# One planner for all engines up to the sweeps; plain fp32 adaLN, tokens turned before they are scaled, the gate third beside heads 1 to 3

## The chip, the core and the metric

The kernel runs on one core of a Trainium2 chip. The metric is the device time of one execution in microseconds, the median of several runs. TensorE (PE) multiplies matrices out of SBUF into PSUM; VectorE (DVE), ScalarE (ACT) and GpSimd (POOL) work on elements, and GpSimd can't read PSUM; SyncE (SP) issues the DMAs. Each engine takes its instructions strictly in the order in which they were issued to it, and waits for the others by semaphores.

## The reference

One layer of a hybrid encoder, for a prompt of 1024 tokens and a sample of 256, D = 1024. All is fp32.

```python
mod = c @ w_ada + b_ada
shift, scale, gate = jnp.split(mod[:, None, :], 3, axis=-1)
h = rms_norm(x, norm_g) * (1.0 + scale) + shift
p = h @ w_in                                   # (tokens, 11 D + 16)
cb, cc, cx, cz, q, k, v, o, mz, gpre, gmerge = split_combined(p)
y_conv = cb * centred_dwconv3(cc * cx, conv_w, conv_b) * jax.nn.silu(cz)
...  # h_fwd, h_bwd: chunkwise mLSTM over q, k, v with the gates gpre, in both directions, 4 heads
hm = hm * lax.rsqrt(jnp.mean(hm * hm, axis=-1, keepdims=True) + EPS)   # hm = h_fwd + h_bwd
y_m = jax.nn.sigmoid(o) * hm * jax.nn.silu(mz)
g_conv, g_mlstm = jnp.split(jax.nn.sigmoid(gmerge), 2, axis=-1)
merged = g_conv * (y_conv @ w_proj_conv) + g_mlstm * (y_m @ w_proj_mlstm)
return x + gate * (merged @ w_out)             # and a last rms_norm
```

## The kernel before

A large product is made of three products of rounded parts: each operand x is split into a high part H (a cast to fp32r) and a low part L = x - H, and HH, HL and LH are added up in PSUM.

**The start.** Five blocks of 128 tokens are loaded, then the first two thirds of `w_ada` in eight blocks of 1 MB (`wa`, five buffers), then the other five token blocks. ScalarE sums the squares (L355), VectorE scales each block by its root mean square (L362), TensorE turns it to channels x tokens (`turn`, L372). `ada(kt)` splits a block of `w_ada` into parts (ScalarE L411, VectorE or GpSimd L412) and multiplies them by the conditions (L425); the last quarter is multiplied as plain fp32 (L418). The result gives a scale `s1` and a shift `shf` for each channel. Tokens 0 to 383 are turned before these are known; the other groups are turned later, and scaled as they leave PSUM (`affine`, L378 and L380).

**Strassen products.** The input projection is done by a seven-product scheme of blocks: K in two halves, tokens in two halves (`b11`, `b21`, `b12`, `b22`), columns in pairs of 128. The moving operands are b11, b21, b22 and four combinations t1 to t4 (made at L1022, split at L1041 and L1044); the weights are combined on VectorE (`comb`, L513) and split on ScalarE (L292) and GpSimd (L293). One product is 24 matrix instructions of 320 columns (`product`, L471). VectorE adds each result to partial sums (`plus`, L543). There are 308 products: eight pairs of merge gates (the first eight products of them are taken ahead, as "corners"), head 0, eight pairs of o and mz (`og_pair`), sixteen of the convolution, heads 1 to 3. `run` is the order by hand: product p, then the turns and deferred steps of the product before (`turn_one`, `deferred`), the taking up of its result, the weights of product p + 2. Three accumulators (`accx`) are in PSUM.

**Beside the products.** `gate_inputs` and `recurrences` make the mLSTM's scalars. `weights` (20 tiles of exponentials) and `thirds` run beside the og pairs. `thirds` makes the last third of adaLN, the output gate, on VectorE: 128 multiply-adds of 128 x 128 (L966), from weight blocks (`wg`, one buffer) and a bias row (`gacc`), with a sum on TensorE and a row stored for each of eight parts. Keys and values are turned to tokens x channels and stored.

**The sweeps.** The mLSTM runs over heads in two directions. Here a planner, `Board`, already orders all engines: each operation has an engine, a duration written in the code, what it reads and writes and a step; `order` takes again and again the engine that can start first, and of its operations those that can start within 0.25 the one of the lowest step. The product `y_conv @ w_proj_conv` is cut into 32 units (`Filler`) that fill TensorE's gaps; `PACE` says how many units are given out up to each step.

**The output.** For each half of the tokens `merge` makes the mLSTM's projection and adds the two, and `finish` multiplies by `w_out` in quarters of 256 columns (L1668 to L1670), adds the residual (`residual`) and norms (`norm_out`).

## Time and profile before

| | us |
|---|---|
| median of 3 runs (lowest to highest) | 1767.04 (1766.39 to 1769.45) |
| the profiled execution's own time | 1767.08 |
| its span, first to last instruction | 1765.1 |
| TensorE busy | 1681.6 |
| VectorE busy | 958.9 |
| GpSimd busy | 696.7 |
| ScalarE busy | 620.4 |

The stages in the profiled execution: adaLN up to 53 us, Strassen products from 53 to 1229, with og pairs from 371, the convolution from 595 and heads 1 to 3 from 989; the sweeps from 1229 to 1527; the output from there on. A stretch's busy time is to be read beside its length: what TensorE lacks there is what an edit of that stretch can win at most. Durations of matrix instructions overlap, so the time of one is read from the distance of two starts.

### The profile page before, as it was taken

To read this page: it belongs to the slowest core of one execution; us is meant where nothing else is said; L and a number is where in the kernel's file an instruction comes from. 1 tells how busy PE (TensorE), PEld (TensorE's weight loads), DVE (VectorE), ACT (ScalarE), POOL (GpSimd) and SP (SyncE) were. 2 spreads that over 40 slices of the span, in tenths; PEclk is the share of its full clock that TensorE was granted. 3 is DMA by queue.
4 is the path that set the end of the run, shared out by engine and by line. 5 is a ranking of instruction groups with operands and counts; after the bars stand their busy time and mean duration, and the time that the engine had idled before them with its cause. 6 is when DMAs were issued, how large, how long until landed. Compare 5 with 4: busy or idle time off the path is not lost.

```text
span 1765.1 us, 29030 instructions
## 1 busy us (share of the span) xinstructions
PE 1681.6 (95%) x11182; PEld 1620.9 (92%) x11182; DVE 958.9 (54%) x1703; ACT 620.4 (35%) x1243; POOL 696.7 (39%) x533
## 2 busy tenths in 40 slices
PE   4879999999988999999999999999999999899997
PEld 1679999999887999999999999999888889799997
DVE  6884333257788455555554433322247677556546
ACT  6552332223444322222222222222246565334223
POOL 2453333334454466666666633333210101223322
PEclk9889999999999999999999999999999999899999
DMA  7223332313554322222222243336878864763731
GB/s 298 84 74 119 108 101 96 106 56 106 150 162 136 97 67 78 58 64 71 66 78 66 89 123 103 96 123 230 295 230 273 271 188 142 252 222 121 255 101 72
DMA packets 213694, 239.59 MB, mean 136 GB/s; under 512 B 12356, under 2 KB 172340, under 8 KB 212532
## 3 DMA queue, kind: packets, MB, share of 16 engines
q1 hardware_dynamic: 213556, 237.74, 42.4%
q8 instruction: 88, 1.44, 0.3%
q14 instruction: 50, 0.41, 0.1%
HBM read 169.46 MB, written 68.23 MB: 135 GB/s over the span
## 4 chain that ended last, share of the span: by engine, by line
PE 63%; DVE 3%; DMA 1%; issue 1%; ACT 1%; POOL 0%; SPq 0%; DVEq 0%; ACTq 0%; POOLq 0%
PE accx L471 36%; PE qc L1281 3%; PE u L1299 3%; PE accd L1454 2%; PE accd L1455 2%; PE accd L1456 2%; PE accd L1669 2%; PE accd L1670 2%; PE accd L1668 2%; PE acc L1523 2%; PE acc L1524 2%; PE acc L1525 2%; PE misc L1382 1%; PE misc L1342 1%; DVE gacc L966 1%
## 5 line engine op out<-in xcount | busy, mean ns | idle before, releaser
L543 DVE TENSOR_TENSOR q<-accx,q 128x640 f32<-128x640 f32 x288 | 233.4, 821 | 477.4 <-PE accx L471 404.7
L293 POOL TENSOR_TENSOR wl<-comb,wh 128x512 fp32r<-128x512 f32 x176 | 236.8, 1347 | 486.8 <-ACT wh L292 439.6
L293 POOL TENSOR_TENSOR wl<-raw,wh 128x512 fp32r<-128x512 f32 x168 | 234.9, 1403 | 162.7 <-ACT wh L292 150.4
L471 PE MATMUL accx<-half,wh 128*128 128x320 f32 x1408 | 266.0, 311 | 6.9 <-ACT wh L292 5.2
L292 ACT CAST wh<-comb 128x512 fp32r<-128x512 f32 x176 | 108.6, 620 | 371.8 <-DVE comb L513 284.9
L471 PEld LDWEIGHTS accx<-half,wh 128*128 128x128 f32 x1408 | 221.4, 189 | 8.5 <-ACT wh L292 5.5
L471 PE MATMUL accx<-half,wl 128*128 128x320 f32 x704 | 161.0, 310 | 0.8 <-POOL wl L293 0.8
L292 ACT CAST wh<-raw 128x512 fp32r<-128x512 f32 (+1 forms) x184 | 119.5, 654 | 71.2 <-PE accd L1670 17.9
L1484 POOL TENSOR_TENSOR wl<-raw,wh 128x512 fp32r<-128x512 f32 x28 | 35.9, 1288 | 234.8 <-ACT wh L1483 234.8
L632 ACT ACTIVATE q<-q,zero 128x640 f32<-128x640 f32 x80 | 66.4, 830 | 172.0 <-DVE q L543 153.7
L471 PEld LDWEIGHTS accx<-half,wl 128*128 128x128 f32 x704 | 118.0, 188 | 1.4 <-POOL wl L293 1.4
L1669 PE MATMUL accd<-wl,mH 128*128 128x256 f32 x320 | 89.6, 280 | 0.1
L1670 PE MATMUL accd<-wh,mL 128*128 128x256 f32 x320 | 89.5, 280 | 0.0
L1668 PE MATMUL accd<-wh,mH 128*128 128x256 f32 x320 | 89.5, 280 | 0.0
L471 PE MATMUL accx<-b10H,wh 128*128 128x320 f32 x352 | 82.5, 316 | 7.0 <-ACT q L1070 5.9
L471 PE MATMUL accx<-t2H,wl 128*128 128x320 f32 x352 | 81.4, 313 | 5.6 <-POOL wl L293 5.6
L471 PE MATMUL accx<-b00H,wh 128*128 128x320 f32 x352 | 82.0, 314 | 2.3 <-DVE half L380 2.3
L471 PE MATMUL accx<-t2H,wh 128*128 128x320 f32 x352 | 81.7, 313 | 2.0 <-ACT wh L292 2.0
L471 PE MATMUL accx<-b10H,wl 128*128 128x320 f32 x352 | 81.2, 312 | 1.1 <-POOL wl L293 1.1
L471 PE MATMUL accx<-t3H,wl 128*128 128x320 f32 x352 | 80.4, 310 | 1.1 <-POOL wl L293 1.1
L471 PE MATMUL accx<-t3H,wh 128*128 128x320 f32 x352 | 80.5, 310 | 1.0 <-ACT wh L292 1.0
L471 PE MATMUL accx<-b11H,wl 128*128 128x320 f32 x352 | 80.3, 309 | 1.1 <-POOL wl L293 1.1
(301 smaller groups left out, 4233.2 us busy)
## 6 DMA issues: line engine op xcount, KB each, us to landing
raw<-in_w_in_dram SPq DMA_DIRECT2D x96, 256.0 KB
raw<-in_w_in_dram SPq DMA_DIRECT2D x44, 512.0 KB
th_dr<-q SPq DMA_DIRECT2D x32, 320.0 KB
th<-th_dr SPq DMA_DIRECT2D x32, 320.0 KB
wa<-in_w_ada_dram SPq DMA_DIRECT2D x8, 1024.0 KB
raw<-in_w_proj_conv_dram SPq DMA_DIRECT2D x16, 512.0 KB
k<-kn_dr SPq DMA_DIRECT2D x64, 128.0 KB
raw<-in_w_proj_mlstm_dram SPq DMA_DIRECT2D x16, 512.0 KB
```

Of the source, the lines that this page charges most:

```text
L292: A.copy(wh[:], src)
L293: eng.tensor_tensor(out=wl[:], in0=src, in1=fp(wh[:]), op=ALU.subtract)
L471: PE.matmul(acc[:, q, 0:TQ], st_[:, k, :], m_[:, q * TQ:(q + 1) * TQ], start=k == 0 and n == 0, stop=k == 3 and n == 2)
L543: V.tensor_tensor(out=two(dst), in0=ps, in1=two(t), op=ALU.add)
L632: A.activation(out, in_, AF.Tanh, bias=zero[:, 0:1], scale=0.5)
L1281: PE.matmul(pq[:, 0:HD + 2], qTs[i][:, kd, c * P:(c + 1) * P], C[:, kd, :], start=kd == 0, stop=kd == 1)
L1299: PE.matmul(pu[:, db, 0:HD + 2], k[:, db * P:(db + 1) * P], wv[:], start=True, stop=True)
L1454: PE.matmul(accs[q][:, :TQ], wh, yH, start=kt == 0, stop=False)
L1484: op("POOL", 1.36, lambda wh=wh, wl=wl, src=src: G.tensor_tensor(out=wl[:], in0=src(), in1=fp(wh[:]), op=ALU.subtract), r=[raw, wh], w=[wl])
L1668: PE.matmul(pd, sH, ws[0][:, k, :], start=kt == 0, stop=False)
L1669: PE.matmul(pd, sH, ws[1][:, k, :], start=False, stop=False)
L1670: PE.matmul(pd, sL, ws[0][:, k, :], start=False, stop=kt == KT - 1)
```

## The change

The planner now orders all engines from the first load on, in pieces with one plan each (`board.play` is called at the end of each, and forgets what it has played); `run`, `defer`, `settle` and the lists of stores are gone. `phase` and `go` record the same 308 products, each in four operations (one for each block of K). `prep` records the weights of a product with the step of two products before (five for the first twelve).

- *The start*: all ten token blocks are loaded before `w_ada`, normed, and turned without scale and shift into the operands' buffers. `w_ada` isn't split: each block is multiplied as plain fp32 (32 products of 512 columns). Then `affine` scales and shifts in place in SBUF, and `both_parts` and `combine` make the seven operands, while the corners run (two of b11, two of b21, then pairs).
- *By tokens*: keys and values are turned as soon as the plan has them.
- *The gate third* (`thirds`) moves from the og pairs to heads 1 to 3: it is recorded at each seventh product, its sum six products later. The heads' ring of result tiles has six tiles instead of eight.
- *Sweeps*: units from 18 on (22 before) have low priority, and `PACE` gives 30 units before step 50 and the last two from it on.
- *Output*: `w_out` in halves of 512 columns: half as many matrix instructions, twice as wide, and the same for the operations of `residual`.

```diff
-                wah = ad.tile([P, D], F32R, tag=f"wah{h}", name="wah")
-                wal = ad.tile([P, D], F32R, tag=f"wal{h}", name="wal")
-                A.copy(wah[:], was[kt][:, hs])
-                (G if h == 0 and kt % 2 == 0 else V).tensor_tensor(out=wal[:], in0=was[kt][:, hs], in1=fp(wah[:]), op=ALU.subtract)
-                parts[h] = wah, wal
...
+        self.ops = []
+        for key in list(self.places):
+            self.places[key] = [b for b in self.places[key] if b.open]
+            if not self.places[key]:
+                del self.places[key]
...
+        def turn_x(i, cs):
+            t0, tn = cs[0] * P, len(cs) * P
+            for kt in range(KT):
+                px = buf(psP, [P, 512], F32, "px", 2)
+                dst, d0 = xt[kt // 4, t0 // TH2][kt % 4], t0 % TH2
+
+                def turn(px=px, kt=kt):
+                    for j, c in enumerate(cs):
+                        PE.transpose(px[:, j * P:(j + 1) * P], xin[c][:, kt * P:(kt + 1) * P], ident[:])
+
+                op("PE", .11 * len(cs), turn, r=[xin[c] for c in cs], w=[px])
+                f = (A.copy, V.tensor_copy)[kt % 2]
+                op(("ACT", "DVE")[kt % 2], .5, lambda f=f, px=px, dst=dst, d0=d0: f(dst[:, d0:d0 + tn], px[:, :tn]),
+                   r=[px], w=[(dst, i)])
...
+        def ada(kt):
+            for h in range(2):
+                for j in range(2):
+                    op("PE", .88, lambda h=h, j=j: PE.matmul(
+                        pada[h][0:4, j, :], cz4[:, kt, :], was[kt][:, h * D + j * 512:h * D + (j + 1) * 512],
+                        start=kt == 0, stop=kt == KT - 1), r=["cz4", was[kt]], w=[("pada", h, j)])
...
+        for i, cs in enumerate(GROUPS):
+            load_x(cs)
+        for kt in range(KT):
+            load_ada(kt)
...
+    def affine(j, l, ks=range(4)):
+        for i in ks:
+            x, kt = xt[j, l][i], 4 * j + i
+            for a, b, smp in ((0, TH2, 0),) if l == 0 else ((0, T0 - TH2, 0), (T0 - TH2, TH2, 1)):
+                sc, sh = s1[:, kt, smp:smp + 1], shf[:, kt, smp:smp + 1]
+                act = i % 2 if l == 0 else smp
...
+    def prep(k):
+        if k < len(todo) and k not in made:
+            board.step = k - (5 if k < 12 else 2)
+            made[k] = todo[k][0].prep(todo[k][1])
...
+        for k_ in range(4):
+            op("PE", .84, lambda k_=k_: mm(k_), r=[*w, *((MOV_B[mv][part][k_]) for part in range(2))] + ([acc] if k_ else []),
+               w=[acc])
+        for b in w:
+            b.open = False
+        take(acc)
...
+            op("PE", .11 * jn, turn, r=[t.tok], w=[pv])
+            op("ACT", .2 + .1 * jn, lambda j0=j0, jn=jn, pv=pv: A.copy(vt()[:, j0 * P:(j0 + jn) * P], pv[:, :jn * P]),
+               r=[pv], w=[(vt.b, j0)])
...
+            op("DVE", .95, first, r=ru, w=rc)
+            op("DVE", 2.0, left, r=ru + rc, w=rc)
+            op("DVE", 2.0, right, r=ru + rc, w=rc)
...
+        for k in range(8):
+            if k == 2:
+                board.step = 3
+                affine(1, 1)
+                affine(0, 1)
+
+                board.step = 4
+                both_parts("b22", B22, (0, 0, 0, 0))
+                combine(B22, B22, B12, 0)
+                board.step = 7
+                combine(B12, B12, B11, 1)
+                board.step = 5
+                combine(B11, B22, B11, 0, ALU.add)
+                both_parts("t2", B11, (0, 0, 0, 0))
+                board.step = 6
+                both_parts("t3", B22, (0, 1, 0, 1))
+                board.step = 8
+                combine(B21, B21, B11, 0)
+                singles("t1")
+                both_parts("t1", B12, (1, 1, 1, 1))
+                singles("t4")
+                both_parts("t4", B21, (0, 0, 0, 0))
...
-            side = [weights(gw), thirds(gw)]
-            run(ends[8], side)
...
+    def thirds(pool, n):
+
+        acc = buf(pool, [P, 2, P], F32, "acc", 2)
+        op("POOL", .45, lambda: G.memset(acc[:], 0.0), w=[acc])
+        for s in range(2):
+            load(1, lambda s=s: acc[0:1, s], b_ada[0:1, 2 * D + n * P:2 * D + (n + 1) * P], [], [acc])
+        for j in range(2):
+            raw = buf(pool, [P, 4, P], F32, "wg", 1)
+            load(256, lambda raw=raw: raw[:], wada[:, 4 * j:4 * j + 4, 2 * D + n * P:2 * D + (n + 1) * P], (), [raw])
+            for i in range(4):
+                def use(i=i, j=j, raw=raw):
+                    for s in range(2):
+                        k = 8 * s + 4 * j + i
+                        V.scalar_tensor_tensor(out=acc[:, s], in0=raw[:, i], scalar=cols[:, k:k + 1], in1=acc[:, s],
+                                               op0=ALU.mult, op1=ALU.add)
+
+                op("DVE", .85, use, r=[raw, acc], w=[acc])
...
+            if n < KT and m == 0:
+                third[n] = thirds(gw, n)
+            if n < KT and m == 6:
+                third[n]()
+            go(k)
...
-    PACE = [min(4 + s, 12) if s < 10 else 12 + (s - 9) * 4 // 7 if s < 17 else 16 if s < 21 else min(17 + (s - 21) * 15 // 29, 32)
+    PACE = [min(4 + s, 12) if s < 10 else 12 + (s - 9) * 4 // 7 if s < 17 else 16 if s < 21 else min(17 + (s - 21) * 13 // 28, 30) if s < 50 else 32
...
-                op("PE", .88, lambda part=part: mm(part), r=ops + ([acc] if part else []), w=[acc], low=u >= 22,
+                op("PE", .88, lambda part=part: mm(part), r=ops + ([acc] if part else []), w=[acc], low=u >= 18,
...
+        def residual(pd, j, n2):
+            ns = slice(n2 * 512, (n2 + 1) * 512)
+            t = ep.tile([P, 4 * P], F32, tag="t", name="t")
             V.tensor_tensor(out=t[:], in0=pd, in1=gbc[0 if c0 + j < 8 else 1][:, ns], op=ALU.mult)
             V.tensor_tensor(out=ob[:, j, ns], in0=ob[:, j, ns], in1=t[:], op=ALU.add)
             A.activation(t[:], ob[:, j, ns], AF.Square, bias=zero[:, 0:1], scale=1.0,
-                         accum_out=ssq[:, j, n4:n4 + 1])
+                         accum_out=ssq[:, j, n2:n2 + 1])
...
+        for n2 in range(2):
+            ws = [weights_o(n2, half) for half in range(2)]
+            if last and n2 == 1:
```

## Rows read from the trace of the kernel before

**Rows 1.** The page: the span, and the engines' busy time with its share of the span.

```profile
span 1765.1 us, 29030 instructions
...
PE 1681.6 (95%) x11182; PEld 1620.9 (92%) x11182; DVE 958.9 (54%) x1703; ACT 620.4 (35%) x1243; POOL 696.7 (39%) x533
```

**Rows 2.** Busy time by stretch, the whole kernel: the stretch and its length in us, busy us (and instructions) of each engine, granted clock as a share of full speed, DMA share, GB/s.

```profile
5.00:24.00 19.00, 6.59 (x24) 3.94 (x24) 8.17 (x27) 11.56 (x19) 0.06 (x1) 1.00 0.99 406
...
53.00:131.00 78.00, 61.89 (x356) 58.53 (x355) 63.85 (x77) 42.30 (x68) 39.20 (x23) 0.85 0.16 52
...
131.00:455.00 324.00, 324.00 (x2221) 320.08 (x2220) 145.99 (x240) 99.01 (x170) 117.68 (x92) 1.00 0.34 101
455.00:580.00 125.00, 110.79 (x700) 101.04 (x699) 105.02 (x172) 51.36 (x115) 63.18 (x53) 1.00 0.54 153
580.00:990.00 410.00, 410.00 (x2798) 410.00 (x2797) 217.80 (x242) 103.37 (x169) 256.71 (x179) 1.00 0.22 68
990.00:1004.00 14.00, 12.07 (x71) 11.55 (x70) 6.56 (x6) 4.94 (x8) 8.57 (x6) 0.88 0.55 189
1004.00:1229.00 225.00, 224.65 (x1561) 224.26 (x1559) 70.31 (x95) 57.75 (x117) 78.41 (x62) 1.00 0.40 128
...
1240.00:1518.00 278.00, 270.41 (x1584) 246.43 (x1583) 174.62 (x574) 145.48 (x377) 37.23 (x29) 1.00 0.72 230
1518.00:1532.00 14.00, 6.71 (x27) 5.83 (x26) 5.75 (x13) 4.18 (x9) 2.00 (x2) 0.63 0.79 248
...
1586.00:1643.00 57.00, 57.00 (x487) 57.00 (x486) 36.07 (x56) 23.59 (x52) 21.17 (x22) 1.00 0.38 121
...
1756.00:1765.00 9.00, 0.00 (x0) 0.00 (x0) 3.91 (x13) 1.62 (x4) 0.72 (x1) 0.75 0.44 176
```

**Rows 3.** The chain that ended last, in order of time, heads 1 to 3: start us, us, what.

```profile
1008.18 10.56 PE accx L471 x72
```

**Rows 4.** TensorE in order of time, 85 to 135 us: start us, us to the end of the last of them, what; in brackets the idle time before and what ended it.

```profile
118.46 1.44 PE L471 MATMUL accx<-half,wh 128*128 128x320 f32 x4 [5.24 <-ACT wh L292]
...
131.12 0.45 PE L471 MATMUL accx<-t2H,wh 128*128 128x320 f32 x2
```

**Rows 5.** TensorE in order of time, from the start to the turns of the last two token groups (columns as in rows 4).

```profile
36.09 1.09 PE L425 MATMUL accx<-wal,cst 128*4 128x512 f32 x4
37.02 1.09 PE L425 MATMUL accx<-wah,cst 128*4 128x512 f32 x4
...
46.02 1.88 PE L418 MATMUL accx<-wa,cz 128*4 128x512 f32 x4
47.83 0.63 PE L425 MATMUL accx<-wah,cst 128*4 128x512 f32 x2
48.30 0.62 PE L425 MATMUL accx<-wal,cst 128*4 128x512 f32 x2
...
53.11 0.54 PE L471 MATMUL accx<-b00H,wh 128*128 128x320 f32 x2
...
73.25 2.34 PE L372 MATMUL accx<-ident,xin 128*128 128x128 f32 x15
```

**Rows 6.** ScalarE in order of time, 0 to 60 us (columns as in rows 4).

```profile
7.55 1.28 ACT L355 ACT_TABLE_LOAD   x1 [7.55 <-DMA xin<-in_x_prompt_dram]
8.84 1.15 ACT L355 ACTIVATE junk<-xin,zero 128x1024 f32<-128x1024 f32 x1
...
10.12 1.15 ACT L355 ACTIVATE junk<-xin,zero 128x1024 f32<-128x1024 f32 x1
...
12.65 1.28 ACT L269 ACT_TABLE_LOAD   x1
...
17.92 0.48 ACT L432 COPY half<-misc 128x384 f32<-128x384 f32 x1 [0.16 <-PE misc L372]
...
50.97 1.02 ACT L378 ACTIVATE half<-misc,shf,s 128x256 f32<-128x256 f32 x2 [0.29 <-DVE shf L454]
```

**Rows 7.** Groups of instructions by line and shape, the whole kernel (the weights' low parts, first row) and 50 to 131 us (the rest): engine, operation, out<-in, shapes xcount | busy us, mean ns of one | idle time before and what ended it.

```profile
L293 POOL TENSOR_TENSOR wl<-raw,wh 128x512 fp32r<-128x512 f32 x168 | 234.9, 1403 | 162.7 <-ACT wh L292 150.4 <-issue 7.2 <-PE accd L1455 4.7
...
L1022 DVE TENSOR_TENSOR half<-half 128x640 f32<-128x640 f32 x12 | 14.4, 1244 | 4.0 <-POOL half L1022 4.0
...
L1044 POOL TENSOR_TENSOR half<-half 128x640 fp32r<-128x640 f32 x4 | 7.8, 1968 | 5.2 <-ACT half L1041 5.2
L1022 POOL TENSOR_TENSOR half<-half 128x640 f32<-128x640 f32 x4 | 7.2, 1837 | 0.0
...
L1044 DVE TENSOR_TENSOR t2L<-half,t2H 128x640 fp32r<-128x640 f32 x4 | 5.7, 1425 | 0.1
...
L1044 DVE TENSOR_TENSOR b00L<-half,b00H 128x640 fp32r<-128x640 f32 x4 | 3.2, 823 | 0.6 <-ACT b00H L1041 0.5
```

**Rows 8.** The same view, the gate third's multiply-adds.

```profile
L966 DVE SCALAR_TENSOR_TENSOR gacc<-wg,cols,gacc 128x128 f32<-128x128 f32 x128 | 65.1, 577 | 17.3 <-DMA gacc<-in_b_ada_dram 10.1 <-DMA wg<-in_w_ada_dram 3.8 <-DMA og_dr<-q 2.1
```

**Rows 9.** Who waited for whom on VectorE, 440 to 580 us: us in total, times, longest.

```profile
DVE gacc L966 <- DMA gacc<-in_b_ada_dram: 10.1, 3, 4.7
```

**Rows 10.** The chain that ended last, its end (columns as in rows 3).

```profile
1757.44 0.33 DVE t L1675
```

**Rows 11.** Groups by line and shape, one of the two steps of the short convolution (columns as in rows 7).

```profile
L712 DVE SCALAR_TENSOR_TENSOR cv<-u,cwh,cv 128x255 f32<-128x255 f32 x8 | 12.1, 1518 | 0.0
...
L712 DVE SCALAR_TENSOR_TENSOR cv<-u,cwh,cv 128x1023 f32<-128x1023 f32 x8 | 10.2, 1272 | 0.0
```

More of the change, by code (lines that the diff above doesn't have):

```diff
@@ L100, in order @@
         for o in self.ops:
+            o.before = {b for b in o.before if not b.played}
             count[o] = len(o.before)
@@ L460, in encoder_kernel @@
     hp1 = hstack.enter_context(tc.tile_pool(name="hp1", bufs=1, side="right"))
[L461 to L473 removed]
+    sstack = ctx.enter_context(ExitStack())
@@ L519, in w_12 @@
         def w_12(self):
-            return split_w(wp, self.block(1, 1), G)
+            return self.split(self.block(1, 1))
         def w_t2(self):
@@ L623, in settle, with e_11 @@
[L623 to L635 removed]
+            then(self.plus(acc, t, t if spent and dst is None else dst))
+        def e_11(self, acc):
+            self.p1 = p1 = new_q()
+            op("ACT", .69, lambda: A.copy(two(p1()), acc[:, :, 0:TQ]), r=[acc], w=[p1.tok])
```

1217 lines of the change are left out of this document (551 added, 666 removed).

## The prediction

> **What bounds the kernel now.** I read the page first: TensorE is busy 95% of the span, VectorE 54% [rows 1]. So the kernel is bound by TensorE, and time can come only from the places where TensorE stands still or runs at the lower of its two clock levels. The busy time by stretch says where these are [rows 2]. Between 131 and 455 us and between 580 and 990 us TensorE is busy without a break, at full clock. Four stretches are not like that. From the start to 131 us: in 53 to 131 us it is busy 61.89 of 78 us at a mean level of 0.85. From 455 to 580 us: 110.79 of 125 us. The border of conv stage and heads, 990 to 1004 us: 12.07 of 14 at 0.88. The sweeps: 270.41 of 278, and their end, 1518 to 1532 us, 6.71 of 14 at 0.63. Then I looked at the work that TensorE must do in any case: three Strassen products in a row take 10.56 us, so one is 3.52 us [rows 3], and 308 of them are done before and after the change alike. The reader is to see that an edit away from those four stretches can hardly win, but can lose.
>
> The sum is made against the profiled execution: its own time is 1767.08 us (span 1765.1 and 2.0 around it), and the median of the runs is 1767.04, so no correction is needed between the two.
>
> **The start, up to the thirteenth product.** Here most of the change lies. Before, the thirteenth product ends at 131.12 us [rows 4], the first begins at 53.11 [rows 5]; 13 x 3.52 = 45.8 us of products fill 78 us. The change removes the split of the adaLN matrix into two rounded parts (a cast on ScalarE and a subtraction for each half) and multiplies it as plain fp32; it turns all ten token blocks while adaLN is loading, and scales and shifts them afterwards in place.
>
> When do the adaLN products begin? They stand in TensorE's queue behind the turns as the plan orders them, and the plan lets ten x blocks land before the matrix. ScalarE must do a square of each x block first: it starts at 7.55, loads its table twice (1.28 each), a square comes each 1.28 us (8.84 to 10.12), a copy is 0.48 [rows 6]. For three of the four groups that is 7.55 + 2.6 + 8 x 1.28 + 12 x 0.48 + 0.9 for three square roots = 27 us. Without that queue TensorE could begin near 20 us, when ten x blocks and the first matrix block (6.3 MB) are down at the 406 GB/s of 5 to 24 us [rows 2], so the bounds are 20 and 30; I take 27. From then on a matrix block lands each 2.6 us at that rate and TensorE needs 3.6 for one, so the loads, x ahead of them in SP's queue, are not what ends last. How long do they take? The plain form appears once in the trace: four instructions, two of the new products, from 46.02 to 47.83 us, so 0.905 each [rows 5]; 32 of them are 29.0 us. (The split form took 0.93 for four, 36.09 to 37.02, so the change makes TensorE's own part of adaLN about two times longer; it wins only because the splits were what was waited for.) Sixteen turns of the last group by 2.34 / 15 = 0.16 are 2.5 us. That makes 58.5 us; 1.5 us for a stretch at the lower level gives 60. From the last adaLN product (48.9) to the first scaled block took 2.1 us [rows 5, 6]; then scale, cast and subtraction of the first block, 2.5 us or so. First product about 65 us, 12 us later than now. Bounds 58 and 70.
>
> From there on everything is turned, so the turns and copies between the products are gone. 65 + 45.8 = 110.8 us if TensorE never waits. What it can wait for is VectorE. Up to the operand t2 (ninth product, wanted at 65 + 28.2 = 93 us) VectorE has for each block: 4 scalings and 6 low parts of b11 and b21, 8 short scalings, 4 low parts of b22, 8 combinations, 4 low parts of t2, 4 results, 2 weight combinations. At 0.82 us for a subtraction that runs alone this is 30 us: ready at 62 + 30 less the last three tiles (2.5) = 89.5, no wait. But the same operation took 1.24 to 1.43 us where GpSimd worked beside it [rows 7]; if all of it did, 45 us, ready at 104.5, an 11 us wait. About half of it meets GpSimd (its low parts of b21, four weight parts, four x1 blocks: 17 of 30 us by 1.97, 1.40 and 1.84 each [rows 7]), so 37 us and a wait of 4. For t1 and t4 (GpSimd's low parts of t1, 1.97 each [rows 7], and 12 tiles that come free one by one) I add 2, bounds 0 and 5, and 1.5 for the lower clock level after the waits. 110.8 + 7.5 = 118.3 against 131.1: **-13 us**, bounds -22 and -3.
>
> A rule of the Trainium skill speaks against this part: "SBUF — State Buffer", section "Who interferes with whom", says that a VectorE instruction with two inputs in SBUF contends with a GpSimd instruction that reads SBUF, and that scalings in place can as well. By [rows 7] the trace agrees (0.82 against 1.24 to 1.43 for one shape). If it caught every operation of this chain, the sum would be 7 us higher, at 1745.
>
> **The gate third.** Between 455 and 580 us TensorE loses 125 - 110.8 = 14.2 us [rows 2]. VectorE is in front of it: 128 multiply-adds of the gate third take 65.1 us [rows 8], and it stands in its queue for the bias row and the weight block, 10.1 us for the bias row in that stretch alone [rows 9], with the evictions of the accumulators behind it. The change puts these 65 us beside heads 1 to 3, where VectorE is busy 70.3 of 225 us [rows 2]: 135 of 225, 60%. The same wait for the bias row may return there, with the same evictions behind it, but three accumulators are some 7 us of cover, and there is room to catch up. With them move 16 loads of 256 KB and some rows through SP's queue, between the stores of k, v and q; the second load of each third waits for the one buffer. **-13 us**, bounds -14.2 and -8.
>
> **The planner in place of hand-written order.** The Strassen stages were an order with a fixed slack of one product before each follow-up; now the planner puts each operation where its own costs say that it can go. About 90 TensorE operations there wait for another engine (64 turns of k and v, the gate inputs, the recurrences, eight sums of the gate third). Cost from the stage that is planned like this already: in the sweeps TensorE loses 278 - 270.4 = 7.6 us [rows 2] over some 290 such operations, 0.026 us each. 90 x 0.026 = **+2 us**. From below 0 (the stretches at 100% can't be bettered), from above by the sweeps' share, 2.7% of the 1098 us from 131 to 1229, 30 us (a rival).
>
> **Border and sweeps.** At 990 to 1004 us 1.9 us of waiting and 12% of clock are lost; other orders of the same work: **-1.5 us**, bounds -3.6 and 0. In the sweeps the pace holds one more unit of filler (3.52 us) back to the last steps and gives the units from 18 on a low priority. The end loses 7.3 us of waiting, and what it does runs at 0.63. A unit more there shortens what comes before by as much: **-3 us**, bounds -8 (the wait and the lower level both go) and +3 (the recurrence is late).
>
> **The output stage.** Twice as wide, half as many products. 487 products of 256 columns take 57.0 us, 0.117 each [rows 2], so 480 are 56.2; the 512 wide ones above took 0.2325, 240 are 55.8. Twice 0.4 is 0.8 us. At the end, VectorE took up the last product late (1757.44, though TensorE had no work from 1756 on [rows 2, 10]), being busy with the block before; with 5.6 instead of 2.8 us for each block it is free by then, some 1.4 us. The operations of the tail double in width, about +0.9, and the last weights' split, whose buffer comes free only as its products are due, costs 0.5 more. **-1 us**, bounds -3 and +2.
>
> Sum: -13 - 13 + 2 - 1.5 - 3 - 1 = -29.5; 1767.1 - 29.5 = 1737.6, say **1738 us**.
>
> **The rivals.**
> - *More of it comes through*: VectorE's chain never delays t2 (no wait, no lower level: -6) and the end of the sweeps fills (-5). 1738 - 11 = 1727. For it: the chain fits at 0.82 each. Against: [rows 7].
> - *The start wins nothing*: the plain product is on TensorE, s1 comes 12 us later, and VectorE's chain begins only then, so the products end at 131 again. For it: the bounds' bad ends (70 us, wait 11, then 5) give 70 + 45.8 + 16 = 132. 1738 + 13 = 1751.
> - *The Strassen stages idle like the sweeps*: 2.7% in place of 2 us: 1738 + 28 = 1766, no difference. For it: it is the same planner. Against: products wait for each other far less than a recurrence does.
> - *Slower*: weights come late in the og and conv stages. The place is GpSimd's queue: its multiplications of conv's u and cv wait there for VectorE, and the low weight parts of the next products are queued behind them. The plan's cost for a conv step is 2.0 us, while one takes 1.27 + 1.52 = 2.8 [rows 11], so VectorE falls behind the plan at each of the eight blocks. Price: where weights came late before (455 to 580 us) 35 products lost 14.2 us, 0.4 each; over the 168 products of og and conv that is 67 us, 1738 + 67 = 1805. It decides from 74 late products on (29.5 / 0.4). Against: GpSimd is busy 256.7 of 410 us there, and weights are made two products, 7 us, ahead.
>
> **How the numbers follow.** Forecast 0.55, more 0.10, nothing at the start 0.17, idle like the sweeps 0.08, late weights 0.10. The predicted time is the forecast's, 1738. The first three are within 1722 to 1757, which holds 0.82. A measurement of this kernel tells about 0.2% (3.5 us) from no change. Faster: 0.55 + 0.10 + 0.17 = 0.82; within 0.2%: 0.07; slower: 0.11 (the last rival and the upper tail of the fourth).
>
> **What would show it.** In the changed kernel's trace: adaLN products begin near 27 us and go on nearly unbroken to 59; the first Strassen product at 65, the fourteenth at 118. A wait of a few us before the ninth product, released by VectorE or ScalarE's cast of t2. No wait over 0.3 us between 450 and 580 us. In the heads VectorE 60% busy and TensorE losing under 3 us. The sweeps' end with less than 5 us of waiting. Wrong would be: many waits of 0.2 to 1 us for weights or turns in the planned stages, a first product after 70 us, or waits for the bias row in the heads.

## The result, and the profile after

The changed kernel takes 1753.58 us (median of 4 runs, 1752.45 to 1756.13), the kernel before 1767.26 beside it (4 runs): ratio 0.9923, 95% interval 0.9906 to 0.9940. It is 13.7 us faster, where 29 were forecast. Its profiled execution has a time of 1753.36 us and a span of 1751.6.

From the page of the changed kernel: span, and busy time of the engines. They answer to [rows 1]: TensorE has 5 us more of busy time in a span that is 13.5 us shorter.

```profile
span 1751.6 us, 27967 instructions
...
PE 1686.7 (96%) x10702; PEld 1596.3 (91%) x10702; DVE 957.3 (55%) x1653; ACT 611.3 (35%) x1201; POOL 693.9 (40%) x511
```

Where did it come from? I lined the two traces up by their products: the start of the same Strassen product in both, from the matmul instructions of TensorE in order of time. Products are counted from 0, so product 13 is the fourteenth.

| stretch | before, us | after, us | difference |
|---|---|---|---|
| start of the trace to product 13 | 131.12 | 134.70 | +3.6 |
| to the first og product | 239.92 | 240.37 | +0.4 |
| og stage | 224.27 | 207.78 | -16.5 |
| conv stage | 394.13 | 394.13 | 0.0 |
| heads 1 to 3, with the border ahead of them | 239.21 | 247.33 | +8.1 |
| sweeps and fillers, to the first merge | 298.52 | 289.93 | -8.6 |
| merges and output, to the last product | 228.64 | 229.05 | +0.4 |
| tail | 9.31 | 8.29 | -1.0 |

The start was to bring 13 us and lost 3.6. Busy time by stretch of the changed kernel (columns as in rows 2, to which they answer):

```profile
65.00:135.00 70.00, 54.51 (x315) 52.82 (x316) 62.41 (x65) 40.76 (x62) 38.52 (x22) 0.83 0.17 56
95.00:125.00 30.00, 16.55 (x76) 15.13 (x75) 28.30 (x21) 13.51 (x21) 24.40 (x13) 0.69 0.15 49
375.00:455.00 80.00, 76.18 (x497) 74.57 (x496) 46.96 (x92) 26.53 (x50) 31.12 (x23) 0.96 0.31 86
455.00:583.00 128.00, 126.74 (x864) 126.40 (x864) 69.06 (x77) 60.73 (x130) 73.45 (x53) 1.00 0.47 135
583.00:977.00 394.00, 394.00 (x2690) 394.00 (x2689) 226.08 (x232) 100.83 (x159) 258.60 (x173) 1.00 0.22 69
977.00:1000.00 23.00, 19.19 (x116) 18.89 (x116) 14.51 (x20) 6.45 (x11) 13.38 (x11) 0.85 0.55 178
1000.00:1224.00 224.00, 224.00 (x1534) 218.79 (x1534) 121.30 (x217) 58.10 (x112) 76.87 (x65) 1.00 0.45 142
1236.00:1505.00 269.00, 263.42 (x1540) 239.72 (x1539) 167.99 (x569) 141.93 (x370) 35.09 (x27) 1.00 0.72 235
1505.00:1520.00 15.00, 11.90 (x76) 10.61 (x75) 7.56 (x18) 6.91 (x17) 3.95 (x3) 1.00 0.61 197
```

The reader is to see five things. Between 95 and 125 us TensorE has work for 16.55 of 30 us, at 0.69 of full clock, while VectorE is busy for 28.30 of them with only 21 instructions. At 375 to 455 us, full before [rows 2], 3.8 us are lost and 4% of clock. From 455 on, where 14.2 of 125 us were lost before, it is 1.3 of 128. VectorE is 54% busy in the heads (60% were expected) and TensorE loses nothing there, but much at the border ahead of it. The sweeps' end loses 3.1 us at full clock where it lost 7.3 at 0.63.

TensorE in order of time, the rows of the changed kernel that answer to [rows 4, 5], and the two new stalls (columns as in rows 4):

```profile
29.30 1.87 PE L405 MATMUL pada<-wa,cz 128*4 128x512 f32 x2
...
66.75 0.56 PE L675 MATMUL acc<-b00H,wh 128*128 128x320 f32 x2 [2.18 <-ACT b00H L840]
...
103.87 0.87 PE L675 MATMUL acc<-t2H,wh 128*128 128x320 f32 x2 [6.59 <-ACT t2H L840]
...
120.72 0.90 PE L675 MATMUL acc<-t2L,wh 128*128 128x320 f32 x2 [4.92 <-DVE t2L L841]
...
134.70 0.45 PE L675 MATMUL acc<-t2H,wh 128*128 128x320 f32 x2
...
383.65 0.65 PE L965 MATMUL misc<-gcol,tri 128*128 128x40 f32 x2 [3.14 <-DVE gcol L957]
...
988.57 0.64 PE L675 MATMUL acc<-t2H,wl 128*128 128x320 f32 x1 [3.81 <-POOL wl L329]
```

The first product begins at 66.75 (forecast: 65). From there to product 13 are 68 us instead of 53. Two waits for parts of t2 alone are 11.5: one before the ninth product (103.87), and one inside it, before its third block of K (120.72), since the plan had put blocks of the next two products in between. VectorE in order of time in front of the second wait:

```profile
108.79 9.79 DVE L846 TENSOR_TENSOR xt<-xt 128x640 f32<-128x640 f32 x5
118.51 2.16 DVE L841 TENSOR_TENSOR t2L<-xt,t2H 128x640 fp32r<-128x640 f32 x1
```

The third low part of t2 stands behind five combinations of some 2 us each. What VectorE and GpSimd did in all that time, groups by line and shape, 65 to 122 us (columns as in rows 7):

```profile
L846 DVE TENSOR_TENSOR xt<-xt 128x640 f32<-128x640 f32 x12 | 20.1, 1714 | 0.0
L859 DVE TENSOR_SCALAR xt<-xt,s,shf 128x384 f32<-128x384 f32 x8 | 6.9, 914 | 0.0
L841 DVE TENSOR_TENSOR t2L<-xt,t2H 128x640 fp32r<-128x640 f32 x4 | 4.9, 1234 | 0.0
```

```profile
L846 POOL TENSOR_TENSOR xt<-xt 128x640 f32<-128x640 f32 x4 | 8.4, 2110 | 2.3 <-DVE xt L846 2.3
L841 POOL TENSOR_TENSOR xt<-xt 128x640 fp32r<-128x640 f32 x4 | 8.2, 2060 | 0.2
```

The combinations (first row) take 1.71 us each, against 1.24 in [rows 7] and 0.81 alone. And here are the engines in front of the two new stalls, VectorE's first operation of the recurrences, GpSimd's first of the gate third, ScalarE's first of the heads:

```profile
378.57 0.24 DVE L935 SCALAR_TENSOR_TENSOR ge<-gcol 128x80 f32<-128x80 f32 x1 [2.48 <-DMA qT_dr<-q]
```

```profile
986.72 0.31 POOL L1066 MEMSET acc<- 128x256 f32 x1 [2.31 <-DMA yc_drL<-cv]
```

```profile
986.68 0.69 ACT L618 COPY q<-acc 128x640 f32<-128x640 f32 x1 [2.97 <-DMA yc_drL<-cv]
```

None of the three reads what that DMA stores. Each is the first user of a new pool, and the reading is that its memory is still being read by a store of the closed pool; e7 and e9 try that.

### The profile page after: what moved, and what is told of

Its sections match the earlier page's. It is cut to its first block, busy times and chain, and to the rows that moved or that the text cites. A ratio compares the mean times of both kernels' runs of the same rounds, so it can differ in the third digit from the quotient of the medians.

```text
span 1751.6 us, 27967 instructions
## 1 busy us (share of the span) xinstructions
PE 1686.7 (96%) x10702; PEld 1596.3 (91%) x10702; DVE 957.3 (55%) x1653; ACT 611.3 (35%) x1201; POOL 693.9 (40%) x511
## 4 chain that ended last, share of the span: by engine, by line
PE 88%; DVE 5%; DMA 3%; issue 2%; ACT 1%; SPq 1%; POOL 0%; DVEq 0%; ACTq 0%; POOLq 0%
PE acc L675 58%; PE qc L1296 3%; PE u L1314 3%; PE accd L1469 2%; PE accd L1470 2%; PE accd L1471 2%; PE accd L1682 2%; PE accd L1683 2%; PE accd L1681 2%; PE pada L405 2%; PE acc L1537 2%; PE acc L1536 2%; PE acc L1538 2%; DVE xt L846 1%; PE misc L810 1%
## 5 line engine op out<-in xcount | busy, mean ns | idle before, releaser
L606 DVE TENSOR_TENSOR q<-acc,q 128x640 f32<-128x640 f32 x292 | 236.7, 821 | 337.0 <-PE acc L675 333.0
L675 PE MATMUL acc<-xt,wh 128*128 128x320 f32 x1408 | 265.7, 311 | 1.2 <-POOL xt L841 1.2
L675 PEld LDWEIGHTS acc<-xt,wh 128*128 128x128 f32 x1408 | 221.8, 189 | 1.7 <-POOL xt L841 1.4
L328 ACT CAST wh<-raw 128x512 fp32r<-128x512 f32 x136 | 83.9, 620 | 272.6 <-PE acc L675 214.0
L675 PE MATMUL acc<-xt,wl 128*128 128x320 f32 x704 | 161.1, 310 | 0.0
L675 PEld LDWEIGHTS acc<-xt,wl 128*128 128x128 f32 x704 | 118.2, 189 | 0.1
L675 PE MATMUL acc<-t2H,wh 128*128 128x320 f32 x352 | 83.1, 318 | 8.4 <-ACT t2H L840 7.2
L675 PE MATMUL acc<-t2L,wh 128*128 128x320 f32 x352 | 82.4, 316 | 5.1 <-DVE t2L L841 5.1
L675 PE MATMUL acc<-t2H,wl 128*128 128x320 f32 x352 | 82.4, 316 | 4.0 <-POOL wl L329 4.0
L675 PE MATMUL acc<-b11H,wh 128*128 128x320 f32 x352 | 81.8, 313 | 0.6 <-DVE q L606 0.6
```

Of the source, the lines that this page charges most:

```text
L328: op("ACT", .63, lambda: A.copy(wh[:], src()), r=r, w=[wh])
L606: op("DVE", .82, lambda: V.tensor_tensor(out=two(dst()), in0=acc[:, :, 0:TQ], in1=two(t()), op=ALU.add), r=[acc, t.tok], w=[dst.tok])
L675: PE.matmul(acc[:, q, 0:TQ], st_[:, k_, :], m_[:, q * TQ:(q + 1) * TQ], start=k_ == 0 and n == 0, stop=k_ == 3 and n == 2)
```

## The experiments

All are edits of the changed kernel and compute the same result. There are two questions: why the start gives nothing (e1 to e3, e5, e6, e9, e10, e12, e13), and what the other stages were worth (e4, e7, e8, e9, e11).

| run | median us | ratio to before, 95% | product 0 | product 13 | product 28 | from 0 to 28 |
|---|---|---|---|---|---|---|
| the changed kernel | 1753.58 | 0.9906 to 0.9940 | 66.75 | 134.70 | 187.96 | 121.2 |
| e1 x1 first | 1749.29 | 0.9881 to 0.9914 | 67.02 | 133.02 | 186.68 | 119.7 |
| e2 all on VectorE, x1 late | 1749.42 | 0.9890 to 0.9922 | 67.16 | 132.33 | 185.11 | 118.0 |
| e3 all on VectorE, x1 first | 1748.06 | 0.9878 to 0.9908 | 67.58 | 132.29 | 185.07 | 117.5 |
| e4 pools on the other side | 1753.64 | 0.9903 to 0.9937 | 67.88 | 136.37 | 189.61 | 121.7 |
| e5 fifth pair's corners | 1745.29 | 0.9857 to 0.9890 | 66.86 | 128.91 | 182.38 | 115.5 |
| e6 other route | 1749.13 | 0.9872 to 0.9901 | 67.38 | 132.55 | 185.38 | 118.0 |
| e7 memory side by side | 1750.77 | 0.9880 to 0.9912 | 67.79 | 136.27 | 189.51 | 121.7 |
| e8 third back in og | 1764.50 | 0.9975 to 0.9996 | 68.10 | 136.66 | 189.91 | 121.8 |
| e9 all parts | 1741.35 | 0.9837 to 0.9866 | 67.68 | 129.51 | 184.79 | 117.1 |
| e10 all parts, old route | 1745.31 | 0.9863 to 0.9896 | 66.86 | 130.99 | 186.26 | 119.4 |
| e11 old pace | 1764.40 | 0.9969 to 0.9988 | 68.46 | 135.97 | 189.63 | 121.2 |
| e12 adaLN split | 1744.97 | 0.9861 to 0.9903 | 61.92 | 129.18 | 182.84 | 120.9 |
| e13 all parts and split | 1735.27 | 0.9808 to 0.9838 | 62.10 | 122.75 | 178.01 | 115.9 |

e4, e7, e8 and e11 leave the order of the start as it is, and yet their product 0 begins up to 1.7 us and their product 28 up to 2.0 us later than in the changed kernel. So differences of that size between two runs' places say little; the distance from product 0 to product 28 repeats better, 121.2 to 121.8 us in these five. A product's number is its place in the order: in e5, e9, e10 and e13 two more corners stand ahead, so their product 13 is another one.

**e1: x1 earlier in the plan.** x1 is written over B12 from B12 and B11; x2 is then written over B11, so it waits for x1's read.

```
-                board.step = 7
+                board.step = 4.5
                 combine(B12, B12, B11, 1)
```

> One number changes: the four x1 blocks (B12 less B11, on GpSimd, written over B12) stand at step 4.5 of the plan, ahead of the low parts of t3 and the weight splits, where they stood at step 7. The block that is read there, B11, is then written over by x2, from which t2 is made. Theory B (the order: x2 waits for x1's read, and x1 for its turn on GpSimd): the waits of TensorE before the ninth and the eleventh product (6.6 and 4.9 us) shrink to under 3 us together, the lower clock level with them, and the fourteenth product begins at 121 to 127 us where it began at 134.7; time 1740 to 1747 us. Theory A (VectorE is the limit, its operations at twice their length beside GpSimd): GpSimd does the same work, only in another order, and VectorE stays busy without a break; the fourteenth product begins within 3 us of 134.7, time 1750 to 1754.

Product 13 moved by 1.7 us, and the distance from product 0 to product 28 fell by 1.5: the order alone (B) falls, as A said. There is now a single wait of 12.3 us before t2, for an accumulator that ScalarE takes up (L618), and those behind it are small; the sum of the waits is no smaller (15.1 us against 13.6).

**e2 and e3: the engine.** In both, x1 and the low parts go to VectorE; e3 has x1 at step 4.5 too.

```
-                combine(B12, B12, B11, 1)
+                combine(B12, B12, B11, 0)
-        both_parts("b21", B21, (0, 1, 0, 1))
+        both_parts("b21", B21, (0, 0, 0, 0))
```

(and the same for t3's and t1's tuples)

> The engine alone: x1, the low parts of b21, of t3 and of t1 (4, 2, 2 and 4 blocks) go from GpSimd to VectorE, x1 still at step 7 of the plan; GpSimd keeps the low weight parts. Theory A (contention): VectorE has 12 operations more (10 us at 0.82) but the combinations fall from a mean of 1.71 to about 1.0 us, and the operand chain is done no later; the waits before products 9 to 11 (14 us together) fall to 5 or less and the fourteenth product begins at 124 to 130 us, time 1743 to 1750. Theory B (the order): x1 still comes behind the low parts of t3 in the plan, only on another queue, x2 still waits for it; waits of 12 us or more stay, time 1751 to 1757.

> Both edits together: x1, the low parts of b21, t3 and t1 on VectorE, and x1 at step 4.5. If order and contention each hold a part, this is the best of the three: the fourteenth product begins at 118 to 124 us (the forecast had 118.3), time 1737 to 1744. If VectorE's own sum of work is what limits (35 of 35 us busy from 88 to 123 us), it is no better than either: fourteenth product 128 to 135 us.

Neither theory gave what it promised: product 13 is at 132.3 in both, 2.4 us earlier, and product 28 is 3.3 and 3.7 us nearer to product 0. It is the last sentence of e3's expectation that came true. Busy time by stretch, e3 (columns as in rows 2), and VectorE in order of time there:

```profile
65.00:135.00 70.00, 56.69 (x338) 54.95 (x337) 62.00 (x80) 43.31 (x65) 20.22 (x13) 0.88 0.20 66
95.00:125.00 30.00, 20.73 (x122) 19.70 (x120) 29.60 (x38) 15.11 (x22) 3.79 (x2) 0.89 0.06 22
```

```profile
92.59 12.15 DVE L846 TENSOR_TENSOR xt<-xt 128x640 f32<-128x640 f32 x12
104.67 3.02 DVE L841 TENSOR_TENSOR t2L<-xt,t2H 128x640 fp32r<-128x640 f32 x4
```

The row of 95 to 125 us is the one to remember. In the same 30 us VectorE did 38 instructions instead of 21, with GpSimd at 3.79 us instead of 24.40, and was busy all the time in both. Twelve operations, some 2.1 us each on GpSimd, went to VectorE, which is busy for 62.0 us from 65 to 135 us afterwards and 62.4 before. So what GpSimd took off VectorE it cost VectorE again, by lengthening the two-input operations beside it from 0.81 to 2.1 us. The Trainium skill's page "SBUF — State Buffer", section "Who interferes with whom", says that only a pair of ports shared by the two engines makes them contend, and that it is an exclusive lock; the trace agrees.

But contention is not the whole bound: with it gone, VectorE is as full. From VectorE's first scaling to its last low part are 56.3 us in e3 (65.95 to 122.23, VectorE busy for 52.2) and 64.6 in the changed kernel (65.12 to 129.74, busy for 58.0), so the operands are complete 7.5 us earlier. TensorE gained less than half of that. Its two longest waits in e3, and ScalarE in front of the first:

```profile
106.14 0.90 PE L675 MATMUL acc<-t2H,wh 128*128 128x320 f32 x2 [7.40 <-ACT q L618]
...
125.98 0.56 PE L675 MATMUL acc<-b11H,wh 128*128 128x320 f32 x2 [2.85 <-ACT wh L328]
```

```profile
102.57 2.93 ACT L840 CAST t2H<-xt 128x640 fp32r<-128x640 f32 x4 [3.42 <-DVE xt L846]
105.41 0.69 ACT L618 COPY q<-acc 128x640 f32<-128x640 f32 x1
```

The first is for an accumulator: ScalarE takes it up behind four casts of t2, which wait for VectorE's combinations. The second is for a weight, whose combination stood in VectorE's queue behind operand parts and three evictions (an eviction takes a result out of its accumulator in PSUM).

**e5: more cover ahead of t2.**

```
-    sts = {n: gate_pair(n, True) for n in range(0, 8, 2)}
+    sts = {n: gate_pair(n, True) for n in range(0, 10, 2)}
```

(and the pair's two products put ahead, its weights loaded with pair 6's)

> The fifth gate pair's two corner products, which need only b11 and b21, are put ahead of the first t2 product: ten products of cover where there were eight (7.0 us), the same 308 products and the same VectorE operations in all. Theory D (VectorE's whole sum of work between s1 at 65 us and t4's low parts at about 120 us comes too late for products that follow each other at 3.52 us): the waits before t2, t1 and t4 (6.6, 1.2, 0.6, 4.9 us) nearly all go, and the half clock level behind them; product 28 begins at 178 to 182 us where it began at 188.0; time 1743 to 1748. Rival B' (a fixed place of x1 in GpSimd's order holds x2 whatever comes before): the waits only move; product 28 at 185 us or later, time 1750 to 1754.

Product 28 is 5.6 us earlier and the time 1745.29: nearly D's numbers, but not D's way. TensorE, the row of the first t2 product:

```profile
116.63 0.60 PE L675 MATMUL acc<-t2H,wh 128*128 128x320 f32 x1 [9.04 <-issue]
```

t2 is two products later in order, yet the wait before it grew to 9 us. The waits after it went. The accumulators of the products before it are evicted on ScalarE at 114.85 and on VectorE at 115.72, both queued behind operand work. So more cover brings the operands no earlier (the last low part ends at 129.8 us, as in the changed kernel), but TensorE does two more products in the meantime. Of the edits of the start that leave s1 (adaLN's scale) where it is, this one won the most.

**e6: fewer combinations ahead of t2.** x2 = B22 - (B12 - B11), and x4 = x2 - B11 after it.

```
-                combine(B22, B22, B12, 0)
+                combine(B12, B12, B11, 0)
...
-                combine(B11, B22, B11, 0, ALU.add)
-                both_parts("t2", B11, (0, 0, 0, 0))
+                combine(B22, B22, B12, 0)
+                both_parts("t2", B22, (0, 0, 0, 0))
```

> The same four combinations by another route, with fewer of them ahead of t2: x1 = B12 - B11 first (on VectorE), then x2 = B22 - x1, which is t2's source, and x4 = x2 - B11 only after it. Eight VectorE combinations stand before t2 where it was eight plus the wait for GpSimd's four (twelve in the run with all of it on VectorE). Theory D (VectorE's sum of work): t2's wait falls from 6.6 to about 2 us, but what is taken from its front comes back before t3 and t1, since VectorE has four combinations more in all; product 28 at 183 to 187 us, time 1746 to 1752. Theory B (only x2's wait for x1 counted): nearly all waits go, product 28 at 177 to 181 us, time 1741 to 1746.

As D said: t2's wait falls to 4.4 us, and 5.1 us come back before t3 and t1.

**e12: adaLN in two rounded parts again**, inside the planner: a cast on ScalarE, a subtraction on VectorE, and products of both parts.

```
-                    op("PE", .88, lambda h=h, j=j: PE.matmul(
-                        pada[h][0:4, j, :], cz4[:, kt, :], was[kt][:, h * D + j * 512:h * D + (j + 1) * 512],
...
+                op("ACT", 1.2, lambda wah=wah, hs=hs: A.copy(wah[:], was[kt][:, hs]), r=[was[kt]], w=[wah])
+                op("DVE", 1.2, lambda wah=wah, wal=wal, hs=hs: V.tensor_tensor(
+                    out=wal[:], in0=was[kt][:, hs], in1=fp(wah[:]), op=ALU.subtract), r=[was[kt], wah], w=[wal])
```

> One part of the change undone, inside the planner: the adaLN matrix is split into two rounded parts again (cast on ScalarE, subtraction on VectorE, both idle for about 17 us there), so that TensorE has about 15 us of adaLN products where the plain form took 34 (29.3 to 63.4 us). s1 is known at 54 to 58 us where it was at 65.1, and the first product begins 7 to 11 us earlier. Theory E (VectorE's 62 us of work behind s1 set the fourteenth product, in whatever order): the fourteenth product and product 28 begin 6 to 11 us earlier too (124 to 129 and 177 to 182); time 1743 to 1748. Rival (something else holds the operands, as weights or loads): the waits before t2 and t4 grow by what the first product gains; product 28 at 185 us or later, time 1750 to 1754.

The first product begins 4.8 us earlier (7 to 11 were expected; TensorE waits for the casts and the subtractions there), product 13 5.5 and product 28 5.1. Everything moves with s1, as E said, and the waits do not swallow it: from product 0 to product 28 are 120.9 us. TensorE, three rows of e12:

```profile
61.92 0.64 PE L683 MATMUL acc<-b00H,wh 128*128 128x320 f32 x1 [2.37 <-ACT b00H L848]
...
98.91 0.60 PE L683 MATMUL acc<-t2H,wh 128*128 128x320 f32 x1 [6.86 <-ACT t2H L848]
...
129.18 0.56 PE L683 MATMUL acc<-t2H,wh 128*128 128x320 f32 x2
```

**e4 and e7: the pools' memory.** e4 only leaves out `side="right"` of the pools gt and gw2; e7 keeps the gate stage's ring of result tiles (6 for 8) through the og stage, with gt beside it, and lets r4 and gw2 wait by tile.

```
-    with tc.tile_pool(name="r1", bufs=8, side="right") as ring[0]:
+    with tc.tile_pool(name="r1", bufs=6, side="right") as ring[0]:
-    with tc.tile_pool(name="r3", bufs=5, side="right") as ring[0]:
...
-    with tc.tile_pool(name="r4", bufs=6, side="right") as ring[0], tc.tile_pool(name="gw2", bufs=1, side="right") as gw:
+    with tc.tile_pool(name="r4", bufs=6, side="right", reuse_waits="tile") as ring[0], \
+            tc.tile_pool(name="gw2", bufs=1, side="right", reuse_waits="tile") as gw:
```

> The pool of the gate recurrences and that of the gate third beside heads 1 to 3 are put on the other side of the memory, where no closing pool's tiles lie. Theory C (the stalls of 3.1 us at 383 us and 3.8 us at 988 us come from tiles that overlap memory which a store of the closing pool still reads, a wait that the plan does not know): both stalls go to under 1 us with the lower clock level behind them (6.8 and 6.9 us at half level), time 1753 less 7 to 13 us, so 1740 to 1747. Rival: the stalls are the recurrences' own chain of small operations between VectorE and TensorE, and GpSimd's queue of weight parts at the border; then both stay, time 1752 to 1755.

> Memory only: the ring of result tiles of the gate stage (six in place of eight) goes on through the og stage, with the recurrences' pool beside it in memory that nobody used; and the two pools of heads 1 to 3 wait for each old tile that they overlap and not for their whole predecessors. (In the earlier run the other side of the memory was occupied too, so nothing was undone there.) Theory C: the first recurrence operation (2.5 us behind the last store of q) and the first third's memset on GpSimd (2.3 us behind the last store of yc) start at once; the stalls of 3.1 us at 383 us and 3.8 us at 988 us fall under 1.5 us each and 3.4 us of lower clock level go at each: time 1744 to 1749. Rival: the chain of small operations and GpSimd's queue set them; they stay over 2.5 us, time 1752 to 1755.

e4 changed nothing, and decides nothing: VectorE's first recurrence operation still waits 2.45 us for the store of q, and GpSimd's first of the third 2.31 us for the store of yc. I take it that the tiles still lay on closed memory; no row shows their addresses. e7, in order of time: VectorE's first recurrence operation, TensorE's wait for the chain, GpSimd at the border:

```profile
377.56 0.23 DVE L935 SCALAR_TENSOR_TENSOR ge<-gcol 128x80 f32<-128x80 f32 x1
```

```profile
382.63 0.64 PE L965 MATMUL misc<-gcol,tri 128*128 128x40 f32 x4 [0.56 <-DVE gcol L957]
```

```profile
984.23 0.31 POOL L1066 MEMSET acc<- 128x256 f32 x1 [2.04 <-DMA yc_drL<-cv]
```

The recurrences' stall is shown: 3.14 us became 0.56, 1.0 us came back later in the chain, and the og stage got 4.1 us shorter (376.62 to 580.35). The border's was not undone (3.56 us): one of the third's two accumulators still waits for cv's store, and so does the first result tile (2.96 us); I take it that both still lay on cv.

**e8: the gate third back beside the og pairs**, now planned.

```
+            for i in range(KT):
+                board.step = at[0] + 5 * i
+                third_ = thirds(gw, i)
+                board.step = at[0] + 5 * i + 5
+                third_()
```

(and its two calls in the heads' loop go)

> The gate third is put back beside the og pairs (pairs 3 to 8, one third each five products), now planned with the rest, and none of it stands beside heads 1 to 3. If its place was the cost (65 us of VectorE work, its queue waiting for the bias row): og loses 8 to 13 us again and the heads win 4 to 8, time 1755 to 1763. If the hand-written order was the cost and the planner finds room for it: og loses under 3 us and the heads win 4 to 8, time 1746 to 1752.

The place was the cost. The og stage takes 230.2 us against 207.8, the heads 239.5 against 247.3, net 14.6. The medians differ by 10.9: the profiled execution of e8 was its slowest, 5.9 us above its median. TensorE, e8, waits for the third's sums, two of four such waits (13.7 us in all):

```profile
463.45 1.01 PE L1083 MATMUL misc<-acc,ones 128*1 128x256 f32 x2 [4.12 <-DVE acc L1076]
...
502.74 0.58 PE L1083 MATMUL misc<-acc,ones 128*1 128x256 f32 x1 [4.65 <-DVE acc L1076]
```

The sum stands five products behind the third's beginning here, six in the heads. Whether a still later sum would cost less in this place was not tried.

**e11: the sweeps' old pace and the old priority of the fillers.**

```
-    min(17 + (s - 21) * 13 // 28, 30) if s < 50 else 32
+    min(17 + (s - 21) * 15 // 29, 32)
...
-    low=u >= 18
+    low=u >= 22
```

> The changed kernel with the sweeps' pace and the filler's priority of before (17 + (s - 21) * 15 // 29, at most 32, low from unit 22 on); nothing else. The sweeps and their end were 8.6 us shorter in the changed kernel, three times the forecast's term. If the pace alone is worth it: time 1759 to 1764. If the rest of the change brought part of it (the gate third's loads out of the way, the first product of the sweeps earlier in hand): 1755 to 1759.

10.8 us slower: the pace and the priority, which this run undoes together, brought the whole gain of the sweeps and a little more. The wait at the sweeps' end is back, in e11's row of TensorE:

```profile
1523.23 0.47 PE L1444 MATMUL misc<-ident,qcf 128*128 128x128 f32 x1 [6.62 <-ACT qcf L1437]
```

**e9, e10 and e13: all parts.** e9 joins e5, e6's route with every operand operation on VectorE, and e7, with the third's tiles where u lay:

```
+            tc.tile_pool(name="gap", bufs=1, side="right", reuse_waits="tile") as gap, \
+        gap.tile([P, T], F32, name="gap")
-    ring[1] = 6
+    ring[1] = 5
```

e10 has the old route of the combinations; e13 is e9 with e12's adaLN.

> What the runs so far point to, together: the fifth pair's corners ahead of t2 (ten products of cover), x1 first and x2 made from it, every operand operation on VectorE so that GpSimd has only low weight parts there, the result ring and the recurrences' pool side by side, and, new, the tiles of the gate third beside heads 1 to 3 put where u lay in the conv stage, with a ring of five, so that none of them overlaps cv, which the closing stores still read. Theory E (a GpSimd operation in SBUF lengthens VectorE's two-input operation beside it by its own length, so moving work to GpSimd buys no time; with neither contention nor due times in the way TensorE hardly waits): waits between products 0 and 28 under 5 us together, product 28 at 170 to 176 us. Theory C at the border: the stall of 3.6 to 3.8 us at 985 us goes below 1 us, and the lower clock level behind it. Time 1726 to 1733 us. If VectorE's sum still holds t2: product 28 at 177 to 181 and 1732 to 1738. If the border stall is the weights' own chain behind GpSimd's multiplications of cv: it stays over 2.5 us, 5 us more.

> As the run of all parts, but with the old route of the combinations (x4, then x1, then x2 in place), all on VectorE: the four x1 stand ahead of x2 again, 3.3 us at 0.82 each. It tells what the new route is worth once nothing contends: product 28 later by 0 to 4 us, time 1726 to 1737, and the same at the border.

> The run of all parts (corners, x1 first, operands on VectorE, memory of the recurrences and the gate third) with adaLN in two rounded parts as well. Theory E: what s1 gains comes off the end: product 28 at 174 to 179 us where it was 184.8, time 1731 to 1736, the fastest so far. If it gains less than 4 us, the start is then held by the loads of x and of the matrix rather than by VectorE.

In e9 the start is a miss: 184.8 where 170 to 176 were expected, and 182.4 with e5's cover alone. TensorE and VectorE there, and the border:

```profile
124.39 0.99 PE L675 MATMUL acc<-xt,wh 128*128 128x320 f32 x4 [2.90 <-DVE q L606]
```

```profile
114.10 9.41 DVE L841 TENSOR_TENSOR xt<-xt 128x640 fp32r<-128x640 f32 x8
123.43 1.55 DVE L606 TENSOR_TENSOR q<-acc,q 128x640 f32<-128x640 f32 x2
```

```profile
978.20 0.56 PE L675 MATMUL acc<-t2H,wl 128*128 128x320 f32 x2 [1.45 <-POOL wl L329]
```

```profile
95.00:125.00 30.00, 20.99 (x128) 19.97 (x127) 29.55 (x36) 16.50 (x24) 12.45 (x4) 0.94 0.18 57
...
969.00:992.00 23.00, 21.21 (x144) 20.71 (x144) 14.92 (x21) 6.92 (x12) 14.82 (x12) 1.00 0.56 177
```

VectorE has no gap from 95 to 125 us; eight low parts stand in its queue ahead of two evictions, and TensorE waits 2.9 us for those. So the operand work on VectorE alone, which brought 3.7 us without the extra cover (e3), cost 3.9 us with it (e10 against e5, from product 0 to product 28). An order with the evictions ahead of the low parts was not tried. The border is settled: with no tile on cv the stall is 1.45 us instead of 3.81 and the clock stays full (0.85 in the changed kernel). The new route is worth some 2 us of the start (e10 against e9), but the two runs' intervals overlap. e13 gained from s1 what E said it would (product 28 6.8 us earlier, time 6.1 less) and is the fastest of all: ratio 0.9823 (0.9808 to 0.9838), 30 us under the kernel before (1765.73 beside it) and about 18 under the changed one.

## Why the prediction went wrong

The direction was right, and 1753.6 is inside the range, near its upper end. That it is inside is in part luck: the sweeps won 5.6 us more than the forecast gave them, and without these the time would be about 1759, above the range's 1757. By its own steps:

- **The start, -13, was +3.6: this is the step that failed.** The first product was right (66.75 for 65), and so was the place of the wait. Wrong were the 7.5 us added to the products' own 45.8 (4 for t2, 2 for t1 and t4, 1.5 for the clock): they were 22.2. Of these, 12.1 are waits for parts of t2 (6.6, 0.6 and 4.9), about what the prediction gave for the case that GpSimd's work lengthened every operation (11); it had taken half of that case, and the combinations took 1.71 us each. Other waits are 1.5. Most of the remaining 8.6 is the lower clock level, some 6 us: the granted clock was 0.83 from 65 to 135 us. Under it lies VectorE: from 65 to 135 us it is busy for 61.8 to 64.1 of the 70 us in the changed kernel and in all runs of the start (53.9 in the kernel before), and its work on the operands begins with s1, which came 14 us later (51 us in [rows 6], 65 here). e12, which moved s1, moved product 13 by as much. That only 3.6 of the 14 were lost fits the turns and copies that no longer stand in between; that was not tried by itself. The order (e1), the engine (e2, e3), the route (e6) and the cover (e5) each won 1.5 to 5.7 us between product 0 and product 28, none of them the 16.4 us that product 13 came after its forecast of 118.3. How much an order of VectorE's queue with the evictions ahead would win stays open. It was the rival "The start wins nothing", at 0.17, and it gave 1751.
- **Contention**, priced at 7 us if it caught everything: it caught the combinations, and the waits for t2 came to that case. With GpSimd's operand work gone the operands were complete 7.5 us earlier, but product 13 only 2.4 (e3), since VectorE then had that work to do and evictions and weights waited behind it.
- **The gate third, -13**: net -14.6 in the profiles (e8), -10.9 by the medians, heads' sums and border included. Right.
- **The planner, +2**: gates +0.4 and conv 0.0, but og has a stall that no sum of small waits shows: 3.14 us, and half clock for some 6 us behind it, together some 6 us. The plan doesn't know that a new pool's tiles lie on a closing pool's (e7, which won 4.1 us of it back).
- **The border, -1.5**: it lost more than before instead, 3.81 us of waiting and clock 0.85, by the same cause (e9).
- **The sweeps, -3, were -8.6**; the pace and the priority are worth 10.8 (e11). The mechanism was right, the size off: at the end the lower level went and the wait fell from 7.3 to 3.1 us, near the bound of -8.
- **The output, -1**: +0.4 and -1.0 in the tail, so -0.6. Right.

So the third (14.6 us by the profiles, 10.9 by the medians) and the pace with the priority (10.8) bring 22 to 25 us, and the rest of the change, the start and the planner's two borders above all, takes 8 to 12 of them back.

## What to carry to other kernels

Before giving a start or a border to TensorE's product count, sum the work of the engine that makes the operands over the whole stretch, up to the last operand and not to the first wait, with the evictions and weights that stand in the same queue, and at the length that the operations have beside the other engine. If that sum fills the stretch, an earlier begin (e12) or other products for TensorE meanwhile (e5) won the most here; another order or engine mostly moved the waits (e1 to e3, e6). A two-input SBUF operation on GpSimd cost VectorE here about as much time as it took off it. And a plan that knows its tiles but not the memory under them will put the first user of a new pool behind the last store of the old one: place the new pool's tiles where nothing late is read.

## What the runs showed of the hardware

A GpSimd operation in SBUF (2.06 to 2.11 us for 128x640) cost VectorE about what the same operation takes on VectorE: in 30 us VectorE did 21 instructions with GpSimd busy for 24.4 us, 38 with it busy for 3.8. It goes the other way too: a low weight part on GpSimd (128x512) takes 1.37 us on average in the changed kernel, and two of them took 8.8 us in e9 (from 111.29 us) beside VectorE's combinations and low parts. At both new stalls of the changed kernel, waits of 3.1 and 3.8 us, TensorE's granted clock was at the 1.2 GHz level for 6.8 us, from 0.9 and 1.6 us before the wait's end on; where the wait was 0.56 or 1.45 us (e7, e9) the clock stayed at 2.4 GHz.
